# Hybrid attention and PEER kernel: sums by products with a ones column, tied gate products, paired one-hots, respread modulation segments

## The chip, the cores and the metric

The kernel runs on one core of a Trainium2 chip. The metric is the device time of one execution in microseconds. A core has TensorE (PE in the profile, its weight loads as PEld), VectorE (DVE), ScalarE (ACT), GpSimd (POOL) and SyncE (SP, which here issues most DMAs); 16 DMA engines move data between the device's memory and the core.

## The reference, cut to what matters

Two layers work on 256 tokens of `x` and 256 context tokens, 1024 wide, in float32. In each layer a conditioning vector gives six modulation vectors per stream; four mixers (latent attention, grouped attention, neighbourhood attention, retention) are merged by gates; then a feed-forward layer picks 16 of 16384 experts for each of 8 heads of a token. The second layer needs no context output.

```python
mx = (jax.nn.silu(c) @ mod_w[l] + mod_b[l])          # six vectors of 1024: sh1, sc1, g1, sh2, sc2, g2
hx = rmsnorm(x, norm1_w[l]) * (1.0 + sc1x) + sh1x
x = x + g1x * hybrid_mixer(hx, ...)
...
# peer_ffn, for a block of 128 tokens
s = jnp.einsum('thpd,hpkd->thpk', q, keys)           # two lists of 128 scores per head
...                                                  # top 16 of each, top 16 of their 256 sums: eidx
g = jax.nn.softmax(top_s, axis=-1)
act = gelu(jnp.einsum('td,thkd->thk', xt, u[eidx]))
return jnp.einsum('thk,thkd->td', g * act, v[eidx])
```

## The kernel before

Nearly all products with weights are made from a high and a low part: a block of 128 x 1024 weights is loaded into `raw` (three buffers), ScalarE copies it to `hi` (L154), VectorE subtracts to `lo` (L157), and TensorE makes three products for each pair of tiles (`hi` by `hi`, `hi` by low, `lo` by `hi`; L358 to L360 and L1229). `hi` and `lo` have five buffers each (`NW`). `split_w` keeps the last such subtraction it has traced in `lo_turn["last"]`.

The order of the instructions of each engine is laid out when the program is built, by the framework's own plan of when operands and buffers come free. `with tc.issue_after(x)` adds one condition to that plan: the instructions of the block stand behind `x` on `x`'s engine. It adds no wait at run time. Each engine then takes its instructions in that order.

A layer has these stages. The mixer (layer 0: about 65 to 560 us) weaves the steps of one branch (`retention`, then three calls of `attention`) with the steps of a second list (`fill_na`, `merge`, `fill_gqa`, `fill_mla`) by a ratio. `with_mods` wraps that second list: after its steps with the numbers in `MODS_AT` (for the three attentions) or in the tuple at L707 (for `retention`) it takes one step of `mods`, the modulation segments. A segment (`mod_seg`) has two halves. For each half and stream, eight loads of 256 KB (`mraw`, two buffers) are multiplied by the conditioning scalars and summed into `macc` of 128 x 512 (first on ScalarE at L250, the other seven on VectorE at L252), so that the sum over partitions is still open. `finish` makes it: TensorE transposes four 128 x 128 pieces into one bank of its accumulator memory (the tag `pt`, one buffer, shared with attention's transposes at L484), VectorE reduces it (L263) and adds the bias (L264). One step of `mods` finishes the half loaded before and loads the next. What is left of `mods` runs after the last `merge`. Layer 0 has six segments and two streams, layer 1 four segments and one.

After the output projection comes the feed-forward layer. It computes the hidden products for all 128 blocks of 128 experts, and multiplies by a dense table of gate weights. `peer_u` (layer 0: about 660 to 1322 us) makes 128 blocks `H`, applies Gelu and stores them to the device's memory (`act_d`, two blocks of 384 tokens together in layer 0, four blocks of 256 tokens in layer 1, where every fourth such tile stays in `keep`). Beside it runs a task list with a cost for each task: routing per tile of 128 tokens, then for each eight tokens `hot` on VectorE, which writes one-hot tables of the two index halves (`a1`, `a2`) and `a1` times the high and the low part of the weight (`bh`, `bl`), and `eight`, in which TensorE multiplies them into 128 x 128 tables that go to `g_d`. In layer 0 one tile of tokens is done by gathers instead: `sparse` gathers one row per token and step (POOL issues them into `gat`, four buffers), and VectorE makes a dot product (L920, first half) or a weighted sum (L930, second half), each behind the last `lo`.

`peer_v` (layer 0: 1322 to 1917 us, layer 1: 2710 to 3056 us) goes over 128 blocks of value weights. Per tile of two (layer 1: four) blocks the stored activations come back as `a` (four buffers in layer 0, two in layer 1), VectorE multiplies them in place by the gate table `G` (L1241, the gate product; two blocks in one instruction), ScalarE makes `wh` and VectorE `wl` (L1245, L1246, three buffers each), and the next `a` is loaded. Then TensorE adds the block into the accumulators (L1229). `G` comes in four chunks for 16 blocks, a group ahead.

Of the kernel before, what the change touches and what calls it, by code (L numbers as in the profile page):

```python
# [11 lines left out]
F16 = mybir.dt.float16  # L12
U32 = mybir.dt.uint32
AF = mybir.ActivationFunctionType
OP = mybir.AluOpType
AX = mybir.AxisListType
# [3 lines left out]
P = 128  # L20
# [10 lines left out]
SP = 1  # L31
NG = 4
AB = (4, 2)
MODS_AT = (((1, 5, 8), (1, 6, 12, 17), (0, 2)), ((1, 8), (1, 12), (2,)))
GS = 16384.0
MLA_SCALE = 96.0 ** -0.5

# [76 lines left out]
def hybrid_peer(ctx, tc, resin, cvec, modw, modb, nw, win, uq, uk, uv, colw, nab, retl, gnw,  # L114
                wbr, wo, wq, keys, ub, vb, urow, fnw, consts, rconsts, rope, out):
    nc = tc.nc
    pe, dve, act, pool, sync = nc.tensor, nc.vector, nc.scalar, nc.gpsimd, nc.sync
# [27 lines left out]
    lo_turn = {"last": None}  # L145

    def inst(x):
        return getattr(x, "ins", x)
# [18 lines left out]
    cons, C = table(cp, "consts", consts)  # L167
    ident = C["ident"]
# [31 lines left out]
    modc, nA, log_decay = {}, {}, {}  # L200
# [41 lines left out]
    def mod_seg(l, s, streams, md, ps_t=None):  # L242
        def load(h):
            acc = {st: md.tile([P, 512], F32, tag=f"macc{st}", bufs=1, name="macc") for st in streams}
            for k in range(KD):
                w = md.tile([P, 512], F32, tag="mraw", bufs=2, name="mraw")
                sync.dma_start(w, modw[l, s, h, k // 2, :, (k % 2) * 512:(k % 2 + 1) * 512])
                for st in streams:
                    if k == 0:
                        act.activation(acc[st], w, AF.Copy, scale=cs[:, k, st:st + 1])  # L250
                    else:
                        dve.scalar_tensor_tensor(acc[st], w, cs[:, k, st:st + 1], acc[st],  # L252
                                                 op0=OP.mult, op1=OP.add)
            return acc

        def finish(h, acc):
            kk = slice(h * 4, h * 4 + 4)
            for st in streams:
                tp = (ps_t or ps_pt)("modt")
                for k in range(4):  # L260
                    pe.transpose(tp[:, k * P:(k + 1) * P], acc[st][:, k * P:(k + 1) * P], ident)
                dst = modc[l][:, s, kk, st]
                dve.tensor_reduce(dst, tp.rearrange("p (k q) -> p k q", k=4), axis=AX.X, op=OP.add)  # L263
                dve.tensor_tensor(dst, dst, modc[l, "b"][:, s, kk], op=OP.add)  # L264
                mod_scale(l, s, h, st)

        a = load(0)
        yield
        finish(0, a)
        a = load(1)  # L270
        yield
        finish(1, a)

    def with_mods(gen, at, mod):
        for i, x in enumerate(gen):
            if i in at:
                next(mod, None)
            yield
# [87 lines left out]
    def weave(main, fill, ratio):  # L366
        owed = 0.0
        for _ in main:
            owed += ratio
            while owed >= 1.0:  # L370
                owed -= 1.0
                if next(fill, fill) is fill:
                    owed = -1e9
        for _ in fill:
            pass

    def mixer(l, hT, st, s_acc, pre):
        full = l == 0
# [158 lines left out]
        for d in range(2):  # L537
# [4 lines left out]
            for pr in range(2):  # L542
                act.activation(qdec[:, pr, d], R["qf"] if d == 0 else R["qb"], AF.Exp,
                               scale=lg[:, 8 + d * 2 + pr:9 + d * 2 + pr])
# [161 lines left out]
                yield  # L706
            yield from proj_tok(B_NV, range(4), lambda t2, p: act.activation(nv[:, t2:t2 + 2, :], p, AF.Copy))  # L707

        weave(retention(), with_mods(fill_na(), (0, 3, 6) if not full else (0, 5), mods), 0.7)
        rs.close()  # L710

        acp = s_acc.enter_context(tc.tile_pool(name=f"acp{l}", bufs=1, reuse_waits="tile", side="right"))
        acc = acp.tile([P, KD, 512], F32, name="acc")
# [219 lines left out]
    def peer_u(l, hT, rp, ap_, pre, kp_, normed, xrow, vps):  # L933
# [30 lines left out]
        def route(tt):  # L964
# [95 lines left out]
            def look2():  # L1060
                if tt not in dense:
                    wn = T[tt, "wn"]
                    spw["idx"] = kp_.tile([P, P], U32, name="idx")
                    spw["wgt"] = kp_.tile([P, P], F32, name="wgt")
                    dve.scalar_tensor_tensor(wn[:, 0], wn[:, 0], float(P), wn[:, 1], op0=OP.mult, op1=OP.add)
                    dve.tensor_copy(spw["idx"], wn[:, 0])
                    dve.tensor_copy(spw["wgt"], wn[:, 2])
                    return
                tp = ps_o("idxT")
                for q in range(3):  # L1070
                    pe.transpose(tp[:, q * P:(q + 1) * P], T[tt, "wn"][:, q], ident)
                ix = up2.tile([P, 4, P], F16, tag="ixT", bufs=2, name="ixT")
                act.activation(ix[:, 0:2].rearrange("p q t -> p (q t)"), tp[:, :256], AF.Copy)
                act.activation(ix[:, 2], tp[:, 256:384], AF.Copy, scale=GS)
                dve.scalar_tensor_tensor(ix[:, 3], tp[:, 256:384], GS, ix[:, 2], op0=OP.mult, op1=OP.subtract)
                T[tt, "ix"] = ix
            add(400, look2)
            if tt not in dense:
# [1 line left out]
            for c in range(8):  # L1080
                def gsub(c=c):
                    T[tt, "stage"] = up2.tile([P, P, 16], F32, tag="gst", bufs=2, name="gst")
                add(0, gsub)
                for j in range(2):
                    def hot(c=c, j=j):
                        t0 = c * 16 + j * 8
                        ix = T[tt, "ix"]
                        cur = [ix[:, q, t0:t0 + 8].rearrange("p (g t) -> p g t", t=2)[:, :, None, :]
                               .to_broadcast([P, 4, P, 2]) for q in range(4)]
                        irep = irep2[:, None].to_broadcast([P, 4, P, 2])  # L1090
                        a2, a1, bh, bl = (up2.tile([P, 4, P, 2], F16, tag=nm, bufs=nb, name=nm)
                                          for nm, nb in (("a2", 2), ("a1", 1), ("bh", 2), ("bl", 2)))
                        dve.tensor_tensor(a2, irep, cur[1], op=OP.is_equal)
                        dve.tensor_tensor(a1, irep, cur[0], op=OP.is_equal)
                        dve.tensor_tensor(bh, a1, cur[2], op=OP.mult)
                        dve.tensor_tensor(bl, a1, cur[3], op=OP.mult)
                        T[tt, "hot", c, j] = a2, bh, bl, T[tt, "stage"]

                    def eight(c=c, j=j):
                        a2, bh, bl, stage = T.pop((tt, "hot", c, j))  # L1100
                        for q in range(2):
                            gp = ps_s("gps")
                            for i in range(4):
                                t = q * 4 + i
                                o = gp[:, i * P:(i + 1) * P]
                                at = a2[:, t // 2, :, t % 2]
                                pe.matmul(o, at, bh[:, t // 2, :, t % 2], start=True, stop=False)
                                pe.matmul(o, at, bl[:, t // 2, :, t % 2], start=False, stop=True)
                            tc0 = j * 8 + q * 4
                            act.activation(stage[:, :, tc0:tc0 + 4],  # L1110
                                           gp.rearrange("p (t i) -> p i t", t=4), AF.Copy)
                        if j == 1:
                            sync.dma_start(g_d[tt * 8 + c], stage)

                    add(2800, hot)
                    if "late" in T:
                        add(0, T.pop("late"))
                    T["late"] = eight
# [70 lines left out]
    def peer_v(l, vp, tail, s_up, keep, sparse_step, gen):  # L1189
# [42 lines left out]
        for e in range(P):  # L1232
            i, q = divmod(e, ng)
            if q % (ng // 4) == 0 and i + 1 < P // ng:
                load_g(i + 1, q // (ng // 4))
            if e % na == 0:
                ia = e // na
                a, G = keep[ia] if ia in keep else loads.pop(ia), loads["G", i]
                for j in range(0, na, 2):
                    a4 = a[:, j:j + 2].rearrange("p j (c t) -> p j c t", t=16)  # L1240
                    dve.tensor_tensor(a4, a4, G[:, :, e % ng + j:e % ng + j + 2].rearrange("p c j t -> p j c t"),  # L1241
                                      op=OP.mult)
                wh = vp.tile([P, na, n], F32R, tag="wh", bufs=3, name="wh")
                wl = vp.tile([P, na, n], F32R, tag="wl", bufs=3, name="wl")
                act.activation(wh, a, AF.Copy)  # L1245
                dve.tensor_tensor(wl, a, wh.bitcast(F32), op=OP.subtract)  # L1246
                nx = ia + AB[l]
                if nx < P // na and nx not in keep:
                    load_a(nx)
            blocks.append(((wh[:, e % na], wl[:, e % na]), next_w(vb[l, e]), e))  # L1250
            if e < P - 4:
                for tt in pacc:
                    accum(e, tt)
            sparse_step()
# [247 lines left out]
```

## Time and profile before

| | |
|---|---|
| Time, median of 3 runs | 3072.34 us (3067.71 to 3074.73) |
| Profiled execution | 3068.09 us, its span 3066.3 us |
| Granted TensorE clock, mean | 0.982 |
| TensorE busy | 2912.8 us, 95% |
| VectorE busy | 2287.7 us, 75% |
| ScalarE busy | 1293.5 us, 42% |
| GpSimd busy | 442.8 us, 14% |
| DMA | 718.42 MB, mean 234 GB/s |

Busy time is the time in which an engine has an instruction in work; a matmul's end is modelled, and neighbours overlap. A wait is idle time of an engine, put down to what ended it. The granted clock is a share of 2.4 GHz: 1.00 is that level, 0.50 is 1.2 GHz, and a mean between them is a stretch that had both.

### The profile page before, as it was taken

The numbers are of one execution on the slowest core, as the hardware profiler recorded it, in microseconds if no ns is written. First come the engines' busy times: TensorE is split into PE (matmuls) and PEld (weight loads), VectorE is DVE, ScalarE is ACT, GpSimd is POOL, SyncE is SP. The second block draws the span as 40 slices with busy tenths as digits, with TensorE's granted clock in tenths as the row PEclk, the third lists the DMA queues.
The fourth block names the chain that finished last, engine by engine and source line by source line (L and its number), as shares of the span: only waits on it lengthen the run. The fifth ranks groups of instructions, "written<-read, shape, count | busy, mean of one in ns | idle before, by whom it ended". The sixth has DMA issues, their size and how long they took to land.

```text
span 3066.3 us, 46551 instructions
## 1 busy us (share of the span) xinstructions
PE 2912.8 (95%) x17771; PEld 2563.2 (84%) x17771; DVE 2287.7 (75%) x4013; ACT 1293.5 (42%) x1910; POOL 442.8 (14%) x378
## 2 busy tenths in 40 slices
PE   8999999799999999998888999999999999999998
PEld 6877767798889989986677777988899999988887
DVE  6768793658989999666666777777659798576665
ACT  6344442433343434332232233545554545554443
POOL 0200011001222232232222322101100000000000
PEclk9999999899999999999999999999999999999999
DMA  6343333435797979998888887465455867898874
GB/s 250 108 145 124 117 124 103 149 116 201 238 331 245 351 258 351 359 380 300 295 303 300 316 275 264 163 211 174 138 167 188 272 213 269 288 312 290 272 257 152
DMA packets 242080, 718.42 MB, mean 234 GB/s; under 512 B 24384, under 2 KB 68544, under 8 KB 236736
## 3 DMA queue, kind: packets, MB, share of 16 engines
q1 hardware_dynamic: 204704, 580.69, 56.1%
q0 software_dynamic: 36864, 134.23, 12.3%
q8 instruction: 139, 2.28, 0.3%
q14 instruction: 85, 0.70, 0.1%
q10 hardware_dynamic: 288, 0.52, 0.0%
HBM read 633.56 MB, written 81.79 MB: 233 GB/s over the span
## 4 chain that ended last, share of the span: by engine, by line
PE 34%; DMA 16%; DVE 15%; issue 4%; ACT 2%; POOL 0%; DVEq 0%; SPq 0%; POOLq 0%; ACTq 0%
PE va L1229 12%; DMA a<-act_d 10%; DVE lo L157 4%; PE H L358 4%; PE H L360 4%; PE H L359 4%; DMA raw<-in_ub_dram 4%; DVE spacc L930 2%; DVE wl L1246 2%; DMA mraw<-in_modw_dram 1%; PE proj L358 1%; PE proj L359 1%; PE proj L360 1%; DVE gat L920 1%; ACT hi L154 1%
## 5 line engine op out<-in xcount | busy, mean ns | idle before, releaser
L154 ACT ACTIVATE hi<-raw 128x1024 fp32r<-128x1024 f32 x676 | 715.7, 1060 | 1345.6 <-DMA raw<-in_vb_dram 451.6
L157 DVE TENSOR_TENSOR lo<-raw,hi 128x1024 fp32r<-128x1024 f32 x680 | 832.2, 1226 | 375.2 <-ACT hi L154 370.9
L358 PE MATMUL H<-h2h,hi 128*128 128x384 f32 (+1 forms) x2048 | 647.9, 316 | 14.7 <-ACT ast L1146 14.7
L360 PE MATMUL H<-h2h,lo 128*128 128x384 f32 (+1 forms) x2048 | 637.1, 312 | 2.5 <-DVE lo L157 2.4
L359 PE MATMUL H<-h2l,hi 128*128 128x384 f32 (+1 forms) x2048 | 637.7, 311 | 0.0
L1229 PE MATMUL va<-lo,wh 128*128 128x512 f32 x1280 | 408.3, 398 | 55.5 <-DVE lo L157 55.1
L358 PEld LDWEIGHTS H<-h2h,hi 128*128 128x128 f32 x2048 | 388.3, 190 | 20.2 <-ACT ast L1146 18.2
L1229 PE MATMUL va<-hi,wh 128*128 128x512 f32 x1280 | 403.4, 394 | 1.6 <-ACT keep L1146 1.5
L1229 PE MATMUL va<-hi,wl 128*128 128x512 f32 x1280 | 402.8, 394 | 0.0
L360 PEld LDWEIGHTS H<-h2h,lo 128*128 128x128 f32 x2048 | 387.6, 189 | 4.1 <-DVE lo L157 3.6
L359 PEld LDWEIGHTS H<-h2l,hi 128*128 128x128 f32 x2048 | 388.6, 190 | 0.0
L1229 PEld LDWEIGHTS va<-lo,wh 128*128 128x128 f32 x1280 | 241.8, 191 | 119.0 <-DVE lo L157 70.3
L1229 PEld LDWEIGHTS va<-hi,wh 128*128 128x128 f32 x1280 | 243.1, 190 | 53.9 <-ACT keep L1146 2.4
L358 PE MATMUL proj<-hh,hi 128*128 128x256 f32 (+1 forms) x808 | 283.1, 351 | 5.3 <-ACT hh L349 3.4
L1229 PEld LDWEIGHTS va<-hi,wl 128*128 128x128 f32 x1280 | 244.0, 191 | 52.0
L359 PE MATMUL proj<-hl,hi 128*128 128x256 f32 (+1 forms) x808 | 276.4, 342 | 0.0
L360 PE MATMUL proj<-hh,lo 128*128 128x256 f32 (+1 forms) x808 | 275.8, 342 | 0.0
L1241 DVE TENSOR_TENSOR a<-a,G 128x768 f32<-128x768 f32 (+1 forms) x112 | 92.2, 842 | 208.6 <-DMA a<-act_d 200.1
L910 POOL DMA_INDIRECT gat<-in_urow_dram,idx x128 | 161.1, 1259 | 536.2 <-DVE gat L920 348.6
L910 POOL DMA_INDIRECT gat<-in_vb_dram,idx x128 | 161.7, 1263 | 412.6 <-DVE spacc L930 396.4
L252 DVE SCALAR_TENSOR_TENSOR macc<-mraw,cs,macc 128x512 f32<-128x512 f32 x224 | 167.4, 781 | 41.2 <-DMA mraw<-in_modw_dram 39.7
L358 PEld LDWEIGHTS proj<-hh,hi 128*128 128x128 f32 x808 | 152.9, 190 | 27.7 <-issue 4.0
(301 smaller groups left out, 4370.4 us busy)
## 6 DMA issues: line engine op xcount, KB each, us to landing
raw<-in_ub_dram SPq DMA_DIRECT2D x256, 512.0 KB, 5.0
raw<-in_vb_dram SPq DMA_DIRECT2D x256, 512.0 KB, 4.9
raw<-in_win_dram SPq DMA_DIRECT2D x112, 512.0 KB, 4.0
mraw<-in_modw_dram SPq DMA_DIRECT2D x160, 256.0 KB, 2.9
g_d<-gst SPq DMA_DIRECT2D x40, 1024.0 KB, 5.5
act_d<-ast SPq DMA_DIRECT2D x64, 384.0 KB, 5.0
a<-act_d SPq DMA_DIRECT2D x64, 384.0 KB, 5.5
G<-g_d SPq DMA_DIRECT2D x32, 768.0 KB, 10.8
```

Source lines behind the costliest of these rows:

```text
L154: act.activation(hi, raw, AF.Copy)
L157: lo_turn["last"] = dve.tensor_tensor(lo, raw, hi.bitcast(F32), op=OP.subtract)
L252: dve.scalar_tensor_tensor(acc[st], w, cs[:, k, st:st + 1], acc[st], op0=OP.mult, op1=OP.add)
L358: pe.matmul(o, a, hh[:, k, c0:c1], start=(k == 0), stop=False)
L359: pe.matmul(o, a, hl[:, k, c0:c1], start=False, stop=False)
L360: pe.matmul(o, b, hh[:, k, c0:c1], start=False, stop=(k == KD - 1))
L910: pool.indirect_dma_start(buf[j], None, urow if j < P else vrow, bass.IndirectOffsetOnAxis(ap=idx[:, k:k + 1], axis=0))
L920: dve.scalar_tensor_tensor(g, g, 1.0, xrow, op0=OP.mult, op1=OP.mult, accum_out=hk[:, 0, k:k + 1])
L930: dve.scalar_tensor_tensor(acc[0], g, hk[:, 1, k:k + 1], acc[0], op0=OP.mult, op1=OP.add)
L1229: pe.matmul(pacc[tt][h], x[:, tsl], y[:, h * 512:(h + 1) * 512], start=(e == 0 and x is wh and y is vh), stop=(e == P - 1 and x is wl))
L1241: dve.tensor_tensor(a4, a4, G[:, :, e % ng + j:e % ng + j + 2].rearrange("p c j t -> p j c t"), op=OP.mult)
L1246: dve.tensor_tensor(wl, a, wh.bitcast(F32), op=OP.subtract)
```

## The change

Four parts. `finish` multiplies the four pieces of `macc` as stationary operands by one column of ones, so that the sums over partitions arrive in four columns, and VectorE adds the bias in one instruction; the reduction goes. The gate products are put behind the last low part traced. `hot` compares both index halves in one instruction of twice the size, for which `ixT` gets another layout (one ScalarE copy more); the two multiplies stay. The steps after which a modulation segment is taken are changed: in layer 0 at the three attentions, one step more in the first; in layer 1 beside `retention`. (The tuple at L707 for layer 0, `(0, 5)`, stays, and so does layer 1's part of `MODS_AT`.)

```diff
-MODS_AT = (((1, 5, 8), (1, 6, 12, 17), (0, 2)), ((1, 8), (1, 12), (2,)))
+MODS_AT = (((1, 4, 7, 11), (1, 6, 11, 16), (0, 3)), ((1, 8), (1, 12), (2,)))
...
                 for k in range(4):
-                    pe.transpose(tp[:, k * P:(k + 1) * P], acc[st][:, k * P:(k + 1) * P], ident)
-                dst = modc[l][:, s, kk, st]
-                dve.tensor_reduce(dst, tp.rearrange("p (k q) -> p k q", k=4), axis=AX.X, op=OP.add)
-                dve.tensor_tensor(dst, dst, modc[l, "b"][:, s, kk], op=OP.add)
+                    pe.matmul(tp[:, k:k + 1], acc[st][:, k * P:(k + 1) * P], C["ones"][:, 0:1], start=True, stop=True)
+                dve.tensor_tensor(modc[l][:, s, kk, st], tp[:, :4], modc[l, "b"][:, s, kk], op=OP.add)
...
-        weave(retention(), with_mods(fill_na(), (0, 3, 6) if not full else (0, 5), mods), 0.7)
+        weave(retention(), with_mods(fill_na(), (0, 4, 8) if not full else (0, 5), mods), 0.7)
...
-                ix = up2.tile([P, 4, P], F16, tag="ixT", bufs=2, name="ixT")
-                act.activation(ix[:, 0:2].rearrange("p q t -> p (q t)"), tp[:, :256], AF.Copy)
-                act.activation(ix[:, 2], tp[:, 256:384], AF.Copy, scale=GS)
-                dve.scalar_tensor_tensor(ix[:, 3], tp[:, 256:384], GS, ix[:, 2], op0=OP.mult, op1=OP.subtract)
+                ix = up2.tile([P, 16, 4, 8], F16, tag="ixT", bufs=2, name="ixT")
+                tq = tp[:, :384].rearrange("p (q c t) -> p q c t", q=3, t=8)
+                act.activation(ix[:, :, 0], tq[:, 0], AF.Copy)
+                act.activation(ix[:, :, 1], tq[:, 1], AF.Copy)
+                act.activation(ix[:, :, 2], tq[:, 2], AF.Copy, scale=GS)
+                dve.scalar_tensor_tensor(ix[:, :, 3], tq[:, 2], GS, ix[:, :, 2], op0=OP.mult, op1=OP.subtract)
...
-                        cur = [ix[:, q, t0:t0 + 8].rearrange("p (g t) -> p g t", t=2)[:, :, None, :]
-                               .to_broadcast([P, 4, P, 2]) for q in range(4)]
-                        irep = irep2[:, None].to_broadcast([P, 4, P, 2])
-                        a2, a1, bh, bl = (up2.tile([P, 4, P, 2], F16, tag=nm, bufs=nb, name=nm)
-                                          for nm, nb in (("a2", 2), ("a1", 1), ("bh", 2), ("bl", 2)))
-                        dve.tensor_tensor(a2, irep, cur[1], op=OP.is_equal)
-                        dve.tensor_tensor(a1, irep, cur[0], op=OP.is_equal)
-                        dve.tensor_tensor(bh, a1, cur[2], op=OP.mult)
-                        dve.tensor_tensor(bl, a1, cur[3], op=OP.mult)
-                        T[tt, "hot", c, j] = a2, bh, bl, T[tt, "stage"]
+                        cur = [ix[:, c * 2 + j, q:q + 2].rearrange("p q (g t) -> p (q g) t", t=2)[:, :, None, :]
+                               .to_broadcast([P, 8, P, 2]) for q in (0, 2)]
+                        irep = irep2[:, None].to_broadcast([P, 8, P, 2])
+                        a = up2.tile([P, 8, P, 2], F16, tag="a12", bufs=2, name="a12")
+                        bb = up2.tile([P, 8, P, 2], F16, tag="bhl", bufs=2, name="bhl")
+                        dve.tensor_tensor(a, irep, cur[0], op=OP.is_equal)
+                        for q in range(2):
+                            dve.tensor_tensor(bb[:, q * 4:q * 4 + 4], a[:, :4], cur[1][:, q * 4:q * 4 + 4], op=OP.mult)
+                        T[tt, "hot", c, j] = a[:, 4:], bb[:, :4], bb[:, 4:], T[tt, "stage"]
...
                 for j in range(0, na, 2):
                     a4 = a[:, j:j + 2].rearrange("p j (c t) -> p j c t", t=16)
-                    dve.tensor_tensor(a4, a4, G[:, :, e % ng + j:e % ng + j + 2].rearrange("p c j t -> p j c t"),
-                                      op=OP.mult)
+                    with tc.issue_after(inst(lo_turn["last"])):
+                        dve.tensor_tensor(a4, a4, G[:, :, e % ng + j:e % ng + j + 2]
+                                          .rearrange("p c j t -> p j c t"), op=OP.mult)
```

## Rows read from the trace of the kernel before

**Rows 1.** page, part 1: busy us, share and instructions of each engine
```profile
PE 2912.8 (95%) x17771; PEld 2563.2 (84%) x17771; DVE 2287.7 (75%) x4013; ACT 1293.5 (42%) x1910; POOL 442.8 (14%) x378
```

**Rows 2.** waits of PE, whole span: us in total, times, longest us
```profile
PE va L1229 <- DVE lo L157: 55.1, 30, 6.5
PE modt L261 <- DVE macc L252: 17.8, 3, 16.3
PE H L358 <- ACT ast L1146: 14.7, 9, 3.7
...
PE modt L261 <- DVE modc L263: 4.2, 3, 2.6
```

**Rows 3.** stretch, PE, PEld, DVE, ACT, POOL busy us, granted clock, DMA share, GB/s
```profile
405.00:540.00 135.00, 134.44 (x650) 102.09 (x651) 79.24 (x152) 49.32 (x91) 21.41 (x15) 1.00 0.34 110
540.00:562.00 22.00, 4.88 (x33) 4.27 (x32) 15.04 (x24) 6.34 (x12) 1.27 (x1) 0.66 0.64 204
830.00:1240.00 410.00, 391.72 (x2675) 377.18 (x2674) 394.46 (x873) 168.02 (x260) 112.42 (x89) 0.99 0.87 310
1240.00:1280.00 40.00, 40.00 (x230) 40.00 (x229) 18.77 (x24) 12.70 (x18) 9.74 (x8) 1.00 1.02 385
1322.00:1917.00 595.00, 538.29 (x2273) 432.82 (x2272) 410.54 (x389) 179.47 (x191) 161.28 (x128) 0.97 0.86 301
2302.00:2640.00 338.00, 335.46 (x3052) 332.56 (x3050) 291.70 (x659) 175.25 (x279) 0.00 (x0) 1.00 0.72 238
2710.00:3066.00 356.00, 347.26 (x1531) 287.08 (x1530) 229.00 (x235) 159.96 (x155) 1.54 (x2) 1.00 0.76 254
```

**Rows 4.** the chain that ended last, in order of time: start, us, what
```profile
1538.46 3.42 DMA a<-act_d
1542.85 1.22 DVE lo L157
...
2710.26 338.99 PE va L1229 x1494
```

**Rows 5.** VectorE from 1533 to 1548 us: start, us, instruction, idle before
```profile
1541.97 0.96 DVE L1241 TENSOR_TENSOR a<-a,G 128x768 f32<-128x768 f32 x1 [1.21 <-DMA a<-act_d]
1542.85 1.22 DVE L157 TENSOR_TENSOR lo<-raw,hi 128x1024 fp32r<-128x1024 f32 x1
1543.98 1.28 DVE L930 SCALAR_TENSOR_TENSOR spacc<-gat,hk,spacc 128x1024 f32<-128x1024 f32 x1
1545.18 0.95 DVE L1246 TENSOR_TENSOR wl<-a,wh 128x768 fp32r<-128x768 f32 x1
```

**Rows 6.** waits of VectorE from 1322 to 1917 us
```profile
DVE a L1241 <- DMA a<-act_d: 175.2, 55, 8.6
```

**Rows 7.** line 1241, 1347 to 1890 us: count, ns min/median/max, first and last start
```profile
L1241 DVE TENSOR_TENSOR a<-a,G x57: 949/959/961, 1347.4 to 1887.4; 128x768 f32<-128x768 f32 x57
```

**Rows 8.** DMA issues, 1347 to 1887 us: count, KB each, us to landing
```profile
raw<-in_vb_dram SPq DMA_DIRECT2D x111, 512.0 KB, 5.5
...
gat<-in_vb_dram,idx POOLq DMA_INDIRECT x120, 6.7
```

**Rows 9.** TensorE from 539 to 562 us: start, us, instructions, idle before
```profile
540.05 1.95 PE L288 MATMUL gp<-consts,modc 128*128 128x128 f32 x16
541.84 0.60 PE L261 MATMUL modt<-consts,macc 128*128 128x128 f32 x4
558.78 1.09 PE L261 MATMUL modt<-consts,macc 128*128 128x128 f32 x4 [16.34 <-DVE macc L252]
```

**Rows 10.** groups of VectorE instructions: count | busy us, mean ns | idle before
```profile
L252 DVE SCALAR_TENSOR_TENSOR macc<-mraw,cs,macc 128x512 f32<-128x512 f32 x224 | 167.4, 781 | 41.2 <-DMA mraw<-in_modw_dram 39.7 <-DVE macc L252 0.4
...
L1093 DVE TENSOR_TENSOR a<-irep,ixT 128x1024 f16<-128x1024 f16 x80 | 54.6, 683 | 10.3 <-PE gps L1108 8.2 <-ACT ixT L1073 2.1
...
L263 DVE TENSOR_REDUCE modc<-modt 128x4 f32<-128x512 f32 x32 | 21.9, 684 | 5.9 <-PE modt L261 5.9
...
L1049 DVE TENSOR_TENSOR oh<-abf,ib 128x2048 bf16<-128x2048 bf16 x12 | 14.6, 1216 | 0.1
```

More of the change, by code (lines that the diff above doesn't have):

```diff
@@ L707, in fill_na @@
             yield from proj_tok(B_NV, range(4), lambda t2, p: act.activation(nv[:, t2:t2 + 2, :], p, AF.Copy))
-        weave(retention(), with_mods(fill_na(), (0, 3, 6) if not full else (0, 5), mods), 0.7)
+        weave(retention(), with_mods(fill_na(), (0, 3, 6) if not full else (0, 4, 8), mods), 0.7)
         rs.close()
@@ L1085, in hot @@
                     def hot(c=c, j=j):
-                        t0 = c * 16 + j * 8
                         ix = T[tt, "ix"]
-                        cur = [ix[:, q, t0:t0 + 8].rearrange("p (g t) -> p g t", t=2)[:, :, None, :]
-                               .to_broadcast([P, 4, P, 2]) for q in range(4)]
-                        irep = irep2[:, None].to_broadcast([P, 4, P, 2])
-                        a2, a1, bh, bl = (up2.tile([P, 4, P, 2], F16, tag=nm, bufs=nb, name=nm)
-                                          for nm, nb in (("a2", 2), ("a1", 1), ("bh", 2), ("bl", 2)))
-                        dve.tensor_tensor(a2, irep, cur[1], op=OP.is_equal)
-                        dve.tensor_tensor(a1, irep, cur[0], op=OP.is_equal)
-                        dve.tensor_tensor(bh, a1, cur[2], op=OP.mult)
-                        dve.tensor_tensor(bl, a1, cur[3], op=OP.mult)
-                        T[tt, "hot", c, j] = a2, bh, bl, T[tt, "stage"]
+                        cur = [ix[:, c * 2 + j, q:q + 2].rearrange("p q (g t) -> p (q g) t", t=2)[:, :, None, :]
[7 more added lines that the diff above has]
+                        T[tt, "hot", c, j] = a[:, 4:], bb[:, :4], bb[:, 4:], T[tt, "stage"]
                     def eight(c=c, j=j):
```

## The prediction

> **What bounds the kernel now.** I read the page first: TensorE is busy 95% of the span [rows 1], so outside its gaps only less TensorE work could help, and the change removes hardly any. The waits of TensorE come second, since they say which gaps there are: 55.1 us behind `lo` (the low part of a weight block), all in the value stage of layer 0, and 17.8 us behind `macc`, of which 16.3 us is one gap [rows 2]. Third, the stretches: layer 0's value stage (1322 to 1917 us) has TensorE at 538 of 595 us, granted clock 0.97 and DMA at 0.86; the same stage of layer 1 has 347 of 356 us; 540 to 562 us has 4.9 of 22 us at a clock of 0.66 [rows 3].
>
> Why `lo` is late stands in the chain in order of time: load `a`, gate product, `lo`, `spacc`, `wl`, next load `a` [rows 4, 5]. VectorE takes its instructions in the order in which they were laid out. There the gate product of the next blocks stands early, waits for its `a` (175.2 us in 55 waits [rows 6]), and two `lo` stand behind it. The load it waits for has only just been issued, at 1538.46, because its buffer was freed by a `wl` standing behind an earlier gate product. So four `a` buffers give one load in flight at a time: the gate products ran ahead and hold the others with finished products. In the stretch shown 57 gate products start between 1347.4 and 1887.4 us, 540.0 / 56 = 9.64 us for a pair of blocks [rows 7].
>
> **The change part by part.** The sum is made against the profiled execution: span 3066.3 us, 3068.1 us with what lies around it, which is 4.2 us below the median of the runs (3072.3).
>
> *Gate products behind the last low part.* Nothing is added but an order: the gate product of pair k now stands behind `lo` of block 2k-1. Behind it on VectorE are `wl` of its pair and the next `lo` and `spacc`; TensorE waits for those, ScalarE (`wh`) for the product. `lo` has five buffers, so block 2k-1's can be made when TensorE has left block 2k-6; the product then comes about five blocks early, and its `a` has been in flight since `wl` of pair k-4. The 175 us stall should go. What is late next, for one pair:
> - TensorE: 36 products at 338.99 / 1494 = 0.227 us [rows 4], 8.17 us.
> - VectorE: 0.96 + 0.95 + 2 x 1.22 + 2.14 x 1.28 = 7.1 us [rows 5]; 2.14 is 120 gathers over 56 pairs [rows 7, 8].
> - DMA: two weight blocks 1.05 MB, `a` 0.39, G 0.39, 2.14 gathers of 0.52 MB, together 2.96 MB. At 301 GB/s for a share of 0.86 a full share moves 350 GB/s [rows 3], 8.45 us. Before this stage it moved 385 GB/s [rows 3], 7.7 us.
>
> I take 8.6 us, a little above the dearer two, since both run near their limit together. That gives 56 x (9.64 - 8.6) = -58 us; the clock that the gaps cost (0.97) comes back inside this. Bounds: -82 us (8.17, TensorE alone) and 0; a loss would need a new wait on `wl`, and the five blocks ahead exclude much of one. The Trainium skill (Perfetto Trace Analysis, Roofline) gives a core's share of memory bandwidth as 358 GB/s, and says that one core alone can go above it. By that figure a pair would take an estimated 8.26 us and this part would be worth at most some 77 us; the 385 GB/s of the stretch before [rows 3] agrees that it can be passed.
>
> In layer 1 the same tie adds an order without a gain: TensorE is at 347 of 356 us there [rows 3]. The tile covers four blocks, the product is ready some three blocks ahead: 0, from -3 to +5.
>
> *Segments spread.* A layer has 12 halves of modulation segments in layer 0, and each step loads the next half after finishing the one before. Now 2 + 3 + 4 + 2 = 11 steps lie in the mixer, so the last half is loaded after the last merge, where nothing covers it: TensorE waits 16.34 us for `macc` at 558.8 and its next four transposes take 1.09 instead of 0.60 us [rows 9]. With 2 + 4 + 4 + 2 = 12 steps that load moves into the last attention, and only the finish is left: -16.3 - 2 x 0.5 = -17 us. What moves: eight 256 KB loads on SP's queue and 14 `macc` steps of 0.78 us [rows 10], 10.9 us of VectorE, into 405 to 540 us, where VectorE is busy 79 of 135 us and DMA 0.34 [rows 3]. Bounds: -18, and -6 if none of the 10.9 us is covered. Layer 1 keeps 3 + 2 + 2 + 1 steps, moved by one or two blocks: 0.
>
> *Sums by products with a ones column.* Out go 32 reductions of 0.684 us [rows 10], 21.9 us of VectorE, in stretches where TensorE is full: 0 for their busy time. The wait of TensorE behind them (second stream, and the shared bank) is 4.2 us, 0.8 of it in the gap just counted [rows 2]: -3 us. 128 transposes become 128 products of one column. Four transposes take 0.60 us, sixteen fp32 products with as many weights and 128 columns 1.95 us [rows 9], 0.15 and 0.12 us each. One column is not in the trace: between free (128 x 0.15 = -19 us) and +4 us (the 0.03 between those two, the other way); I take 0, the nearest row being the product of the same kind with the same weights' shape.
>
> *One-hots in pairs.* Per eight tokens two compares of 0.683 us become one of 2048 elements, for which the 16-bit compare at L1049 takes 1.216 us [rows 10]; the multiplies stay. 2 x 0.683 - 1.216 = 0.15 us, 48 times in layer 0: -7.2 us of VectorE, which is busy 394 of 410 us there while TensorE is busy 392 [rows 3] and waits 14.7 us for `ast` [rows 2]. Both are near the limit: -4, between -7 and +2. In layer 1 VectorE has 46 us to spare [rows 3]: 0. The Trainium skill (VectorE: DVE Perf Modes, What auto-detection actually checks) lets a two-source instruction run two results a cycle when every operand is 16-bit with step 1 innermost. The merged operand keeps its pair of tokens innermost, and L1049 agrees with 1.216 us for 2048 elements; this lowers the chance of the rival below. One ScalarE copy more per tile: 0.
>
> Sum: -58 - 17 - 3 - 4 = -82 us, 2986 us for the profiled execution, 2990 us against the median.
>
> **The rivals.**
> 1. DMA takes the place of the stall. Weight loads have three buffers and land in 5.5 us (median), gathers in 6.7 us [rows 8]; if these lengthen as the share rises, `hi` waits and the share stops short of full. At 0.92, midway from 0.86 towards a share just under full, 322 GB/s make 9.18 us a pair: -26 instead of -58, 3022 us. For it: the forecast needs 8.45 / 8.6, a share of 0.98, with weights, `a`, G and gathers on the same engines; against it: 385 GB/s at 1.02 earlier [rows 3].
> 2. The tie does not do what it says. `lo` itself can run ahead, so a gate product may still stand in front of a load just issued. Then only the other parts remain, -24 us: 3048 us. Against it: the load would need to be later than four pairs of blocks.
> 3. Slower: the paired one-hots lose the 16-bit rate because one operand now spans two tables. At the fp32 rate (1.22 us for 1024 [rows 5]) a group costs 4 x 1.22 = 4.88 instead of 2.73 us, +2.15. In layer 0 that is 48 x 2.15 = 103 us, of which the idle 16 us of VectorE [rows 3] take some: +87; in layer 1 69 - 46 = +23. With the other parts' -78 this is +32: 3104 us. It decides from about 2 us more per group. For it: two operands change shape; against it: the same shape of innermost pair runs at the fast rate today.
>
> **How the numbers follow.** Forecast 0.66 (2966 to 3012), rival 1 0.18 (3012 to 3035), rival 2 0.07 (3035 to 3060), rival 3 0.05, the rest 0.04 for a smaller loss of order, such as TensorE waiting for `wl`, about the time before. The range 2962 to 3030 leaves out rivals 2 and 3, part of rival 1, and a little at the fast end, about 0.2. A measurement of this kernel can tell 0.2% (6 us) from no change: faster 0.92, the same 0.03, slower 0.05.
>
> **What would show it.** In layer 0's value stage: waits of VectorE for `a` near zero, loads of `a` issued some pairs before their product, 8.2 to 8.9 us a pair, waits of TensorE behind `lo` under 15 us, DMA share 0.93 or more, granted clock 0.99. Rival 1 shows as `hi` and TensorE waiting for weight loads that land in 8 us and more; rival 2 as the old stall. At the end of layer 0's mixer: no gap over 3 us before the first `wo` product. The reductions of L263 gone and no TensorE wait behind `modc`. Paired compares at 1.2 us and multiplies at 0.68 us; 2.4 us would be rival 3. The forecast is wrong if the stage still takes over 570 us, or if layer 1's value stage grows by more than 5 us.

## The result, and the profile after

The changed kernel takes 2981.64 us (median of four runs, 2980.28 to 2984.03). The kernel before, beside it, takes 3070.03 us (3065.66 to 3074.73). The ratio is 0.9713, with a 95% interval of 0.9695 to 0.9730: 88 us less, where 82 were forecast. The forecast of 2990 us lay 8 us above it, and the range of 2962 to 3030 holds it.

One line of the diff ahead of the prediction was copied wrongly, and the prediction counted with the wrong line. The changed kernel reads `(0, 3, 6) if not full else (0, 4, 8)` at L707. Layer 1 keeps its `(0, 3, 6)`. It is layer 0 that gets a third step beside `retention`, so its mixer has 3 + 4 + 4 + 2 = 13 steps, not 12, and even the last half is finished inside it. The layout of 12 steps was run as well (e8 below).

By stages, from the first starts of their products: layer 0's value stage went from 611.8 to 529.3 us, its hidden stage from 656.2 to 654.2, and layer 1, up to the end of its last value product, from 1123.1 to 1121.5. The first output product (`wo`) of layer 0 starts at 561.5 us, as before (561.4). So the gain is the value stage's, and the second large term of the forecast, 17 us in layer 0's mixer, does not show.

The page of the changed kernel: busy time and instructions, the rate of data in 40 equal slices of the span, and the shares of the chain that ended last.

```profile
PE 2900.2 (97%) x17899; PEld 2571.7 (86%) x17899; DVE 2272.1 (76%) x3901; ACT 1296.6 (43%) x1917; POOL 504.3 (17%) x378
...
GB/s 243 123 154 124 152 94 86 142 120 176 217 324 280 307 298 294 375 370 365 380 371 369 368 339 150 191 211 152 157 176 199 275 206 273 294 295 288 276 273 151
...
PE 77%; DVE 11%; DMA 6%; ACT 3%; issue 3%; POOL 0%; SPq 0%; POOLq 0%; ACTq 0%; DVEq 0%
```

TensorE has 128 instructions more than before [rows 1]. Slices 19 to 23 (74.5 us each) lie inside the value stage of layer 0, at 365 to 380 GB/s. The stretches, with the columns of [rows 3]:

```profile
405.00:540.00 135.00, 133.16 (x665) 96.18 (x664) 76.72 (x152) 53.06 (x101) 21.17 (x16) 1.00 0.28 88
540.00:562.00 22.00, 22.00 (x107) 18.17 (x106) 6.56 (x8) 6.66 (x10) 4.46 (x4) 1.00 0.25 74
830.00:1240.00 410.00, 390.21 (x2655) 376.70 (x2653) 391.55 (x827) 165.22 (x259) 120.91 (x88) 0.98 0.86 310
1321.00:1850.00 529.00, 529.00 (x2361) 438.33 (x2360) 429.50 (x422) 186.73 (x201) 205.69 (x130) 1.00 0.93 339
1341.00:1714.00 373.00, 373.00 (x1647) 308.87 (x1646) 303.77 (x280) 131.79 (x138) 163.00 (x98) 1.00 1.00 370
1352.70:1817.60 464.90, 464.90 (x2053) 384.97 (x2052) 387.86 (x361) 165.97 (x173) 194.79 (x120) 1.00 0.97 355
...
164.00:171.00 7.00, 7.00 (x35) 7.00 (x35) 4.63 (x8) 1.10 (x2) 0.00 (x0) 0.51 0.28 83
```

The value stage has no idle time left on TensorE: 529 of 529 us at a granted clock of 1.00, where [rows 3] had 538 of 595 at 0.97. 540 to 562 us is full, and the 17 us that stood idle there before are gone, yet `wo` starts no earlier: the time went into the mixer ahead of it. The row of 164 to 171 us is read further down.

Waits of TensorE over the whole span:

```profile
PE gps L1105 <- ACT gst L1108: 13.3, 8, 3.3
PE H L356 <- ACT ast L1144: 9.2, 7, 3.1
...
PE modt L261 <- DVE macc L252: 2.6, 2, 2.0
...
PE modt L261 <- DVE modc L262: 2.3, 2, 1.4
```

The row that led [rows 2], `va` behind `lo` with 55.1 us, is not in this list any more, and `macc` fell from 17.8 to 2.6 us. Waits of VectorE in the value stage, 1321 to 1850 us:

```profile
DVE lo L157 <- ACT hi L154: 91.6, 67, 7.8
DVE wl L1245 <- ACT wh L1244: 2.4, 2, 1.3
```

The 175.2 us behind `a` [rows 6] are gone altogether. VectorE now idles behind `hi`, and that costs nothing, since TensorE is full. VectorE in the same stretch that [rows 5] show, start, us, instruction:

```profile
1539.63 1.21 DVE L157 TENSOR_TENSOR lo<-raw,hi 128x1024 fp32r<-128x1024 f32 x1
1540.76 1.27 DVE L928 SCALAR_TENSOR_TENSOR spacc<-gat,hk,spacc 128x1024 f32<-128x1024 f32 x1
1541.96 0.94 DVE L1240 TENSOR_TENSOR a<-a,G 128x768 f32<-128x768 f32 x1
1543.08 1.23 DVE L157 TENSOR_TENSOR lo<-raw,hi 128x1024 fp32r<-128x1024 f32 x1 [0.18 <-ACT hi L154]
```

The gate product stands behind a `lo` now and starts without a wait. The same line over the stage, and the loads issued meanwhile (1347 to 1820 us; count, KB, us to landing):

```profile
L1240 DVE TENSOR_TENSOR a<-a,G x59: 942/949/954, 1352.7 to 1817.6; 128x768 f32<-128x768 f32 x59
```

```profile
raw<-in_vb_dram SPq DMA_DIRECT2D x117, 512.0 KB, 6.1
a<-act_d SPq DMA_DIRECT2D x55, 384.0 KB, 6.4
G<-g_d SPq DMA_DIRECT2D x24, 768.0 KB, 13.1
gat<-in_vb_dram,idx POOLq DMA_INDIRECT x121, 7.7
```

That is (1817.6 - 1352.7) / 58 = 8.02 us from one gate product to the next, against 9.64. The gate products gain about a pair of blocks on TensorE in this time: TensorE, full throughout, makes 2053 products in the same 464.9 us (the row of 1352.7 to 1817.6 us above), which is 8.15 us for the 36 of a pair. Each load paired with the product that reads it, the load is issued 28.6 us (median) before its product, where it was 5.3 us. Weights, `a` and gathers land 0.6 to 1.2 us later than before, and `G` 4 us later, but TensorE waits for none of them. Two of the rows of before ([rows 8] has the others):

```profile
a<-act_d SPq DMA_DIRECT2D x56, 384.0 KB, 5.2
G<-g_d SPq DMA_DIRECT2D x24, 768.0 KB, 9.1
```

VectorE's groups that the change touched, with the columns of [rows 10], and TensorE's group of the modulation sums:

```profile
L1094 DVE TENSOR_TENSOR bhl<-a,ixT 128x1024 f16<-128x1024 f16 x160 | 102.8, 684 | 1.0
L1092 DVE TENSOR_TENSOR a<-irep,ixT 128x2048 f16<-128x2048 f16 x80 | 97.4, 1219 | 11.2 <-PE gps L1106 8.3 <-ACT ixT L1073 2.8
...
L262 DVE TENSOR_TENSOR modc<-modt,mb 128x4 f32<-128x4 f32 x32 | 5.0, 156 | 19.6 <-PE modt L261 19.5
```

```profile
L261 PE MATMUL modt<-consts,macc 128*128 128x1 f32 x256 | 31.7, 245 | 6.1 <-DVE macc L252 2.6 <-DVE modc L262 2.3 <-DVE ol L678 1.1
```

128 products of one column are 256 instructions. TensorE's timeline (start, us, instructions, idle before) shows what a `finish` costs:

```profile
121.47 0.95 PE L261 MATMUL modt<-consts,macc 128*128 128x1 f32 x8
122.27 0.47 PE L647 MATMUL reto<-vz,Dt 128*128 128x128 f32 x2
...
163.45 1.36 PE L261 MATMUL modt<-consts,macc 128*128 128x1 f32 x8 [0.93 <-DVE modc L262]
...
559.84 1.95 PE L286 MATMUL gp<-consts,modc 128*128 128x128 f32 x16
561.54 0.36 PE L875 MATMUL wo<-hi,ah 128*128 128x256 f32 x1
```

Four products take 0.95 us at the full clock; the four transposes in their place took 0.60 [rows 9].

### The profile page after: what moved, and what is told of

It reads as the page before. It is cut to its first block, busy times and chain, and to the rows that moved or that the text cites. A ratio compares the mean times of both kernels' runs of the same rounds, so it can differ in the third digit from the quotient of the medians.

```text
span 2980.8 us, 46557 instructions
## 1 busy us (share of the span) xinstructions
PE 2900.2 (97%) x17899; PEld 2571.7 (86%) x17899; DVE 2272.1 (76%) x3901; ACT 1296.6 (43%) x1917; POOL 504.3 (17%) x378
## 4 chain that ended last, share of the span: by engine, by line
PE 77%; DVE 11%; DMA 6%; ACT 3%; issue 3%; POOL 0%; SPq 0%; POOLq 0%; ACTq 0%; DVEq 0%
PE va L1227 29%; PE H L356 7%; PE H L358 7%; PE H L357 7%; DMA raw<-in_ub_dram 4%; PE proj L356 4%; PE proj L357 4%; PE proj L358 4%; DVE lo L157 2%; DVE macc L252 1%; PE sc L462 1%; PE attno L495 1%; ACT hi L154 1%; DMA mraw<-in_modw_dram 1%; PE ptp L482 1%
## 5 line engine op out<-in xcount | busy, mean ns | idle before, releaser
L1227 PE MATMUL va<-lo,wh 128*128 128x512 f32 x1280 | 397.6, 389 | 0.0
L908 POOL DMA_INDIRECT gat<-in_urow_dram,idx x128 | 172.9, 1351 | 519.5 <-DVE gat L918 331.7
L908 POOL DMA_INDIRECT gat<-in_vb_dram,idx x128 | 205.3, 1604 | 276.9 <-DVE spacc L928 255.9
L298 POOL TENSOR_TENSOR rs<-rs,mhalf 128x1 f32<-128x1 f32 x16 | 10.1, 634 | 963.2 <-DVE rs L295 927.8
```

Of the source, the lines that this page charges most:

```text
L298: pool.tensor_tensor(r[:, 1:2], r[:, 0:1], mhalf, op=OP.pow)
L908: pool.indirect_dma_start(buf[j], None, urow if j < P else vrow, bass.IndirectOffsetOnAxis(ap=idx[:, k:k + 1], axis=0))
L1227: pe.matmul(pacc[tt][h], x[:, tsl], y[:, h * 512:(h + 1) * 512], start=(e == 0 and x is wh and y is vh), stop=(e == P - 1 and x is wl))
```

## The experiments

Two sets ran, on two chips. In the first (e1 to e4) the kernel before had a median of 3059.51 us (3048.14 to 3064.03), in the second (e5 to e8) 3056.42 us (3045.62 to 3071.66). The changed kernel repeated its median within 1 us from the first measurement to e1, and the kernel before did not (3070, then 3060 and 3056), so differences from the kernel before are read inside one set.

**e1, the changed kernel again**, without an edit, as the mark for e2 to e4.

> The changed kernel as it is, as the reference point of the three runs beside it. Both theories: ratio to before 0.971, about 2982 us.

It took 2981.05 us (2978.41 to 2985.27), 0.9753 of the kernel before (0.9732 to 0.9775): 78.5 us less in this set.

**e2, the sums by transposes again**, all else as changed:

```diff
-                    pe.matmul(tp[:, k:k + 1], acc[st][:, k * P:(k + 1) * P], C["ones"][:, 0:1], start=True, stop=True)
-                dve.tensor_tensor(modc[l][:, s, kk, st], tp[:, :4], modc[l, "b"][:, s, kk], op=OP.add)
+                    pe.transpose(tp[:, k * P:(k + 1) * P], acc[st][:, k * P:(k + 1) * P], ident)
+                dst = modc[l][:, s, kk, st]
+                dve.tensor_reduce(dst, tp.rearrange("p (k q) -> p k q", k=4), axis=AX.X, op=OP.add)
+                dve.tensor_tensor(dst, dst, modc[l, "b"][:, s, kk], op=OP.add)
```

> The changed kernel with the sums made as before (four transposes, reduction on VectorE). Theory: the products with a ones column cost TensorE two passes of 0.11 us where a transpose costs one, 128 x 0.11 = 14 us over both layers, and this ate most of the 16.3 us gap at the end of layer 0's mixer; so this kernel is 8 to 14 us faster than the changed one, about 2970 us, with the first wo product of layer 0 near 548 us. Rival: the steps moved into full stretches ate the gap; then this kernel equals the changed one within 3 us.

It took 2971.98 us (2969.14 to 2976.77), 0.9721 (0.9699 to 0.9743): 9.1 us less than e1, and the runs of the two do not overlap. So the products with the ones column lose time. The group of the sums in e2, and the mixer up to the first `wo` in e2 and then in e1 (columns of [rows 3]):

```profile
L261 PE MATMUL modt<-consts,macc 128*128 128x128 f32 x128 | 19.7, 276 | 7.5 <-DVE modc L263 4.6 <-DVE macc L252 1.5 <-DVE ol L680 1.4
```

```profile
65.00:547.00 482.00, 475.13 (x2528) 365.90 (x2528) 350.15 (x628) 199.13 (x360) 67.43 (x53) 1.00 0.37 123
```

```profile
65.00:560.00 495.00, 487.78 (x2630) 380.96 (x2629) 338.79 (x604) 201.17 (x362) 67.87 (x54) 0.99 0.36 120
```

e1 needs 13 us more up to there, and 487.78 - 475.13 = 12.65 of them are busy time of TensorE, with 102 instructions more; its idle time is the same (7 us in both). VectorE saves the reductions in e1 (338.79 against 350.15 us) and gains nothing by it. The first `wo` came at 547.2 us in e2, 14.3 before the changed kernel's. The hidden stage behind it took 658.0 us in e2 and 653.5 in e1, which takes 4.5 us of that back.

**e3, the steps of before**, all else as changed:

```diff
-MODS_AT = (((1, 4, 7, 11), (1, 6, 11, 16), (0, 3)), ((1, 8), (1, 12), (2,)))
+MODS_AT = (((1, 5, 8), (1, 6, 12, 17), (0, 2)), ((1, 8), (1, 12), (2,)))
...
-        weave(retention(), with_mods(fill_na(), (0, 3, 6) if not full else (0, 4, 8), mods), 0.7)
+        weave(retention(), with_mods(fill_na(), (0, 3, 6) if not full else (0, 5), mods), 0.7)
```

> The changed kernel with the steps of the modulation segments as before (11 in layer 0). Theory: the steps are worth their gap; it returns at the end of layer 0's mixer (14 to 18 us of TensorE idle) and the kernel is 12 to 18 us slower than the changed one, about 2996 us. Rival (the moved steps cost as much as the gap): the same as the changed one within 3 us, 2982 us.

It took 2996.75 us (2991.17 to 3007.26), 0.9813 (0.9789 to 0.9837): 15.7 us more than e1, again without overlap. TensorE's timeline in e3 has the gap of [rows 9] back:

```profile
564.22 1.84 PE L261 MATMUL modt<-consts,macc 128*128 128x1 f32 x8 [14.56 <-DVE macc L252]
566.31 1.86 PE L261 MATMUL modt<-consts,macc 128*128 128x1 f32 x8 [0.26 <-DVE modc L262]
```

The eight instructions take 1.84 us behind the gap instead of 0.95. The spread steps are worth their gap; the prediction's 17 us were right in kind and nearly in size.

**e4, the tie alone**, on the kernel before:

```diff
-                    dve.tensor_tensor(a4, a4, G[:, :, e % ng + j:e % ng + j + 2].rearrange("p c j t -> p j c t"),
-                                      op=OP.mult)
+                    with tc.issue_after(inst(lo_turn["last"])):
+                        dve.tensor_tensor(a4, a4, G[:, :, e % ng + j:e % ng + j + 2]
+                                          .rearrange("p c j t -> p j c t"), op=OP.mult)
```

> The kernel before with the gate products tied behind the last low part, nothing else. Theory: the value stage of layer 0 takes 529 us as in the changed kernel and nothing else moves, 82 us less than before: 2988 us, ratio 0.973. Rival: part of the stage's gain comes from the other parts (VectorE freed by the paired one-hots, a later start): then the stage takes 545 us or more here and the ratio is 0.978 or more.

It took 2983.78 us (2981.73 to 2987.11), 0.9759 (0.9738 to 0.9781): 75.7 us less than the kernel before, within 3 us of the whole change. The hidden and the value stage of layer 0 in e4:

```profile
664.00:1326.00 662.00, 624.91 (x3968) 605.62 (x3967) 593.28 (x1443) 249.56 (x372) 159.85 (x130) 0.97 0.80 286
1326.00:1855.00 529.00, 529.00 (x2360) 438.32 (x2359) 428.99 (x422) 186.89 (x201) 220.07 (x130) 1.00 0.92 340
```

The value stage is the changed kernel's to the microsecond, 83 us less than before. The hidden stage took 662.8 us in this execution, 6.6 more than before, about the difference between 83 and 75.7.

**e5, single one-hots**: the old `ixT` of `[P, 4, P]` and the four instructions of 1024 elements, all else as changed:

```diff
-                        dve.tensor_tensor(a, irep, cur[0], op=OP.is_equal)
-                        for q in range(2):
-                            dve.tensor_tensor(bb[:, q * 4:q * 4 + 4], a[:, :4], cur[1][:, q * 4:q * 4 + 4], op=OP.mult)
+                        dve.tensor_tensor(a2, irep, cur[1], op=OP.is_equal)
+                        dve.tensor_tensor(a1, irep, cur[0], op=OP.is_equal)
+                        dve.tensor_tensor(bh, a1, cur[2], op=OP.mult)
+                        dve.tensor_tensor(bl, a1, cur[3], op=OP.mult)
```

> The changed kernel with the one-hots made singly as before (four instructions of 1024 elements instead of one of 2048 and two of 1024). Theory: VectorE is the fuller engine in layer 0's hidden stage (831 to 1240 us), so 48 x 0.15 = 7 us more there make the kernel 3 to 7 us slower than the changed one, 2984 to 2988 us. Rival: the stage is set by late weight loads and TensorE; then the same within 3 us.

It took 2983.63 us (2976.51 to 2991.64), 0.9756 (0.9729 to 0.9784), which can't be told from e1 or from e6 of its own set. Its stretch of the one-hots:

```profile
831.00:1240.00 409.00, 388.08 (x2640) 373.77 (x2640) 388.75 (x864) 165.85 (x257) 109.87 (x87) 0.99 0.86 307
```

```profile
L1091 DVE TENSOR_TENSOR a<-irep,ixT 128x1024 f16<-128x1024 f16 x80 | 54.9, 686 | 10.7 <-PE gps L1106 8.3 <-ACT ixT L1071 2.4
```

Two compares of 686 ns against one of 1219 save 0.15 us for eight tokens, as worked out. But VectorE is as busy in this stretch with either form (388.75 of 409 us, 391.55 of 410), and TensorE too (388.08, 390.21). The 3 to 7 us did not show; with runs that spread over 15 us, a loss of a few us can't be excluded either.

**e6, two `a` buffers with the tie** (`AB = (4, 2)` to `(2, 2)`, all else as changed):

> The changed kernel with two buffers for a in layer 0's value stage instead of four. Theory: the tie alone broke the loop; a load then still leads its product by two pairs of blocks, 16 us, more than it takes to land (6.4 us median), so the kernel is at most 8 us slower than the changed one. Rival: the four buffers carry the stage; with two the products wait for their loads again (60 us and more of VectorE waiting for a) and at least half of the 82 us is lost, 3020 us or more.

It took 2981.34 us (2972.37 to 2989.49), 0.9757 (0.9722 to 0.9791). The value stage:

```profile
1312.00:1841.00 529.00, 529.00 (x2360) 438.31 (x2359) 429.91 (x422) 187.49 (x201) 203.98 (x130) 1.00 0.93 340
```

With the products in their place, two buffers feed TensorE as fully as four: a load is issued 12.5 us (median) before its product and lands in time.

**e7, two `a` buffers without the tie** (the same edit of the kernel before):

> The kernel before with two buffers for a in layer 0's value stage. Theory: without the tie one load is in flight at a time whatever the number of buffers, since gate products that ran ahead hold the others; the time stays within 10 us of before. Rival: the waits of before come from too few buffers for the landing time; then half of them makes the stage at least 40 us longer.

It took 3068.73 us (3056.45 to 3080.58), 1.0038 (1.0015 to 1.0061): 12 us more than the kernel before beside it, a little over what my theory allowed and far from the 40 of its rival. Waits of VectorE in its value stage (1329 to 1925 us, as long as the stretch of [rows 6]), and the stretch:

```profile
DVE a L1241 <- DMA a<-act_d: 167.7, 58, 9.2
```

```profile
1329.00:1925.00 596.00, 540.89 (x2262) 434.91 (x2263) 417.08 (x395) 181.02 (x193) 161.36 (x129) 0.96 0.87 305
```

Without the tie two buffers stall about as long as four (175.2 us [rows 6]), and a load is issued 4.9 us before its product. The value stage takes 615.1 us, 3.3 more than with four; the hidden stage took 663.9 us, 7.7 more, in this execution. So it was the place of the instruction and not the number of buffers that left one load in flight.

**e8, transposes and the 12 steps** (e2, and `else (0, 5)` at L707), which has layer 0's steps as the prediction read them, with the sums as before:

> The changed kernel with transposes and reduction as before and layer 0's two steps beside retention, (0, 5), as before; the attentions' new steps stay (12 steps, so the last half's load lies in the last attention and only its finish stands after the last merge). Theory: the retention stage, 10 us longer with a third step in the changed kernel, gets part of that back: 2966 to 2972 us, at least as fast as the kernel with transposes alone. Rival: the work moved out of retention costs the same elsewhere, 2972 us; or the finish after the last merge opens a gap again, 2980 us.

It took 2969.77 us (2966.19 to 2978.66), 0.9718 (0.9689 to 0.9746), the fastest of all and level with e2; its median is 12 to 14 us below those of e5 and e6 beside it (2983.63 and 2981.34, neither told from the changed kernel), though some of the runs overlap, and 86.7 below the kernel before. TensorE at the end of its mixer:

```profile
544.13 0.60 PE L261 MATMUL modt<-consts,macc 128*128 128x128 f32 x4
544.57 1.95 PE L288 MATMUL gp<-consts,modc 128*128 128x128 f32 x16
546.35 0.60 PE L261 MATMUL modt<-consts,macc 128*128 128x128 f32 x4
546.71 0.36 PE L877 MATMUL wo<-hi,ah 128*128 128x256 f32 x1
```

The last finish stands here without a gap, at 0.60 us for four, as the prediction had it for 12 steps. The thirteenth step is worth nothing measurable.

## Why the prediction came out right, and where it did not

**The gate products.** The chain that the prediction read from [rows 4 to 6] held at each link. The wait for `a` went to nothing, loads are issued 28.6 us ahead (more than three pairs), TensorE's wait behind `lo` went, the clock is 1.00. e4 shows that the tie alone does it, e6 and e7 that the number of buffers has next to no part in it. The size was off. The step that failed is the choice of 8.6 us a pair, "a little above the dearer two", with 8.45 us for DMA from 350 GB/s at a full share. The pair took 8.15 us of TensorE, whose own price was put at 8.17, so the true value lay at the end of the range called "TensorE alone" (-82): -82.5 us by the stage, -75.7 by e4's time, and the pair just under the 8.2 to 8.9 us named as the sign of success. DMA moved 339 GB/s at a share of 0.93 over the stage, or 339 / 0.93 = 365 for a full share, and 370 at a share of 1.00 from 1341 to 1714 us, where the 2.96 MB of a pair take 8.0 us. Both engines ran near their limit together, and neither cost the other anything that shows. The rate per share of the stalled stage thus understated what a fed stage gets; why a share is worth more there was not tested. The Trainium skill (Perfetto Trace Analysis, Roofline) puts a core's share at 358 GB/s and lets one core alone go above it; the profile's slices of 365 to 380 GB/s agree with the second half, and the 8.26 us a pair worked out from the first was 0.1 us too long.

**The steps.** Forecast -17, measured -15.7 (e3 against e1). The count of steps behind it was wrong by one, as told above, and e8 shows that this did not matter.

**The sums by products.** This step failed in its sign: forecast -3 with nothing for TensorE and +4 as the worst for its products, measured +9.1 (e2 against e1). The bound read sixteen instructions of `gp` in 1.95 us as sixteen products. They are eight: L286 (L288 before) makes four products for each half, and each fp32 product is two instructions, as the 256 instructions for 128 products show; a transpose is one. Each of these instructions has a weight load of its own (256 loads, where e2 has 128); whether the loads set the price was not tested. A product thus takes 0.95 / 4 = 0.24 us against 0.15, with one column as with 128; from start to start, without the end of the last one, it is 0.20 (121.47 to 122.27 us for four) against 0.11 (544.13 to 544.57 in e8). The 0.12 us that the prediction read for a product was half of one. For 24 finishes of layer 0, at 0.95 against 0.60 us each, that is 24 x 0.35 = 8.4 us, laid on an engine that is full. Of the wait that was to go with the reduction, 4.2 us behind `modc`, 2.3 stayed. e2's mixer was 12.65 us of TensorE shorter. Of the other 4 us, 3.4 are the clock: summed over stretches of 4 us, what the granted clock lacked to 1.00 in the mixer comes to 5.1 us in e1 and 1.7 in e2, one execution of each. In the profiled execution of the changed kernel the granted clock is also 0.51, the 1.2 GHz level for nearly all of 164 to 171 us, right behind a finish with 0.93 us of waiting; e1 has such a stretch there too and e2 has none there. But e3, with the ones column and the old steps, has none there either, and the kernel before has 0.57 from 134 to 138 us; that such stretches come from the ones column is not shown. The Trainium skill (TensorE: Matmul & The Clock Gate, Terms) calls the transpose mode four times faster for FP32. The direction agrees; the factor here is 0.24 / 0.15 = 1.6 (1.8 from start to start), at 128 columns for the transpose and one for the product. The rule speaks against this edit, and the prediction did not weigh it.

This is why the mixer shows no gain: 16.3 us of gap went, and with the sums by products the first `wo` came 12.9 us later (e1 against e2).

**The one-hots.** Durations as forecast (1219 and 684 ns), worth not -4 but nothing that e5 could tell; the bounds +2 to -7 are not contradicted. VectorE and TensorE near their limits here did not mean that 7 us less of one is 7 us less of the stage.

**Layer 1.** Forecast 0, measured -1.6 over the whole layer; its `va` products run from 2621.8 to 2971.1 us, 349.3 us, against 349.8 before.

**The sum.** -75.7 - 15.7 + 9.1 + 0 = -82.3 by the experiments, -78.5 measured beside them. The forecast had -82 as well, but by two errors that cancel: the tie was worth 18 us more than said, and the sums and the one-hots 16 less. That the total came so near is luck; the mechanism of the largest term is not.

**The rivals.** DMA did not take the stall's place, though it was full (a share of 1.00) for most of the stage: loads of weights land in 6.1 us, and TensorE waits for none. The tie did what it says. The paired compares kept their rate (1219 ns, not 2.4 us).

**Open.** The hidden stage of layer 0 took 647 us (e6) to 664 us (e7) over the profiled executions, which shifts differences of whole kernels by 5 to 8 us (e2, e4, e6, e7) without an edit that is meant for it. TensorE idles 29.3 us of it in e6 and 39.5 in e7; what sets this was not found. Nor was it found why the kernel before has medians of 3070, 3060 and 3056 us in three sets (e1 to e4 and e5 to e8 ran on different chips) while the changed one stays at 2981.

## What to carry to other kernels

When an engine waits for a load, look at when that load was issued before adding buffers: here an early place in an in-order engine's list held four buffers so that one load was in flight, and one condition on the order was worth 76 us, where half the buffers cost the value stage 3 us without the condition and nothing with it. Price a fed stage by each engine's own work, not by a rate taken while the stage was starved. And before work is moved from an engine with slack to the one that bounds the kernel, count that engine's instructions for it: a product that looks like one column can cost more than the transpose that it replaces.

## What was not expected of the hardware

- An fp32 product of one column takes two TensorE instructions and 0.24 us (eight instructions in 0.95 us), as long as one with 128 columns (sixteen in 1.95 us); the fp32 transpose of 128 x 128 is one instruction and takes 0.15 us (four in 0.60 us).
- The 16 DMA engines moved 365 to 380 GB/s over some 370 us of the value stage (370 at a share of 1.00 from 1341 to 1714 us), and per full share 365 in the mean of the stage, where the starved stage before gave 350.
- A stretch of 7 us at a granted clock of 0.51 stands in the middle of a busy mixer (164 to 171 us), right behind a wait of 0.93 us; the 2.35 us that TensorE idled before 148.3 us were followed by a clock of 1.00. What sets such a stretch off was not found.
